# Where the two halves of a split weight chunk and the features start in SBUF: one tile per chunk, placed by the width of the matmuls that use it

## The chip, the cores and the metric

One core of one Trainium2 chip runs the whole program in one launch. The metric is the device time of that core in microseconds (us), the median of several runs. TensorE (PE) multiplies; its weight loads are shown apart as PEld; ScalarE (ACT), VectorE (DVE), GpSimd (POOL) and SyncE (SP, which issues the DMAs) work beside it.

## The reference, cut to what matters

Two blocks of layers on one sequence of 512 tokens with 1024 features, everything in float32:

```python
# first block
x = x + (rms(retention(q, k, v)) * silu(gate)) @ w_out          # 4 heads, after rmsnorm(x) @ w_in
x = x + (softmax_with_sink(q k^T + bias, window 128) v * silu(gate)) @ w_out   # 16 heads ("swa")
# second block, for i in 0, 1
x = layer_norm(ALPHA * x + (mlstm_mixer(x) if i == 0 else pool_mixer(x)))
x = layer_norm(ALPHA * x + memory_cross_attn(x, mem_k, mem_v, wq, wo))
x = layer_norm(ALPHA * x + (relu(x @ w1 + b1) ** 2) @ w2 + b2)   # 1024 -> 4096 -> 1024
```

Nearly all of it are products of [512, 1024] features with weight matrices.

## The kernel before, in words

The features of all 512 tokens lie in SBUF, feature-major, 128 features to a k-tile. Every float32 operand is split into two float32r parts, `hi` (a rounding copy by ACT, L120) and `lo` (the rest, `src - hi`, by DVE, L121), and one product becomes three matmuls (`mm3`, L220 to L222): hi·hi, hi·lo and lo·hi. Each of the three has a weight load (LDWEIGHTS) of 128 columns of its own, so weight load and matmul alternate all through the program: while one matmul streams its moving operand from SBUF, the weight load for the next one reads its stationary operand from SBUF.

Weights come in chunks of one megabyte ([128, 2048] float32). `load` brings a chunk into a `raw` tile by DMA and splits it into a tile `whi` and a tile `wlo` of 8192 bytes per partition each; `chunk` has the next two chunks split ahead of the one in use. `raw` has two places, `whi` and `wlo` three each, taken in turn. During the sliding-window layer one of the three places of `whi` is held for the keys (`kT`).

There are two widths of matmul. In 512-column matmuls the moving operand is either 512 tokens of features (`proj` over the whole sequence: `mm<-xh,whi` in the trace, first the moving and then the stationary operand) or 512 columns of weights (`out_block`, with 128 tokens of features as the stationary operand: `mm<-whi,hh`). In 256-column matmuls it is 256 columns of weights (`tproj`, `mm<-whi,xh`) or half of the tokens (`mm<-xh,whi` with 256). A scheduler sets the order of the instructions on each engine from its own model of their times; tile pools set the addresses.

Where the operands start follows from the built program. All starts here are byte addresses within a partition, modulo 512; every k-tile and every block of 128 columns begins a whole number of 512 bytes further on, so one number stands for a tile:

| Tiles, before | start modulo 512 |
|---|---|
| `whi`, `wlo`, `xh`, `xl`, `kT` | 352 |
| retention's and mLSTM's `q, k, v, p, oh, ol, yh, yl` | 192 |
| the swa layer's `swa_oh, swa_ol, pT, vz` | 288 |
| cross attention's `mk, mv, o01, o23`, `xp`, and the MLP's `hh, hl` | 160 |

"Distance" below means: start of the stationary operand that is loaded during a matmul, less start of the moving operand that this matmul streams, modulo 512. Counted over the built program of before, pair by pair in PE's order, the float32r matmuls have these distances: of 512 columns 2732 at 0, 1912 at 320, 571 at 352 and 196 at 448; of 256 columns 3718 at 0, 211 at 320, 205 at 192 and 140 at 448. The groups in the trace: `mm<-xh,whi` is at 0 in both widths, and so are `mm<-whi,xh` and `mm<-xph,mvh`; `mm<-whi,hh` at 320 with 512 columns and `mm<-whi,o23h` at 320 with 256; `mm<-whi,oh` at 352; `mm<-kT,swa_oh` at 448 and `mm<-o23h,whi` at 192 (both 256).

Of the kernel before, what the change touches and what calls it, by code (L numbers as in the profile page):

```python
# [10 lines left out]
F32 = mybir.dt.float32  # L11
F32R = mybir.dt.float32r
# [3 lines left out]
PSUM = bass.MemoryType.PSUM  # L16

P = 128
# [15 lines left out]
# columns of the packed per-feature vectors  # L34
# [8 lines left out]
# columns of the packed shape-only constants  # L43
# [8 lines left out]

class Ring:
    """a tile pool whose tags hand out their places in turn"""
# [4 lines left out]
    def tile(self, shape, dt, tag, name, bufs=None):  # L59
        n = bufs or self.bufs  # L60
        k = (self.turn.get(tag, -1) + 1) % n
        if k == self.held.get(tag):
            k = (k + 1) % n
        self.turn[tag] = k
        return self.pool.tile(shape, dt, tag=f"{tag}{k}" if n > 1 else tag, name=name, bufs=1)

    def hold(self, shape, dt, tag, name):
        """the next place, kept out of the turns until it is let go"""
        t = self.tile(shape, dt, tag, name)
        self.held[tag] = self.turn[tag]  # L70
        return t

    def let_go(self, tag):
        del self.held[tag]


class Net:
    def __init__(self, ctx, tc, a, out, stop, start):
# [5 lines left out]
        self.wp = pool("w", 3)  # L84
        self.xp = pool("x", 1)
        self.sp = pool("small", 2)
# [4 lines left out]
        # residual stream, token-major  # L91
# [31 lines left out]
    def split_scaled(self, hi, lo, src, sc):  # L123
        """the same of sc * src"""
# [21 lines left out]
    def load(self, name, i, g=None):  # L146
# [4 lines left out]
        elif name == "pool_w":  # column c of group g scaled by pool_scale[g, c]  # L151
            raw, hi, lo = self.wtiles(name, 0)
            sc = self.wp.tile([P, 2048], F32, tag="raw", name="pool_sc", bufs=2)[:, :D]
# [5 lines left out]
        elif g is not None:  # row k * 128 + p scaled by g[p, k]  # L159
# [10 lines left out]
    def order(self, names):  # L170
        """the weight chunks of the phases, in the order of their use"""
# [37 lines left out]
    def wtiles(self, name, i):  # L209
        raw = self.wp.tile([P, 2048], F32, tag="raw", name=self.uid("raw"), bufs=2)  # L210
# [13 lines left out]
    def proj(self, ck, j, x, sl, kt=8, ps=None):  # L224
        """feature-major projection: features j*128.. of the chunk, tokens sl"""
# [7 lines left out]
    def tproj(self, ck, x, blk, ps):  # L233
        """token-major projection of one token block, 256 features of the chunk"""
# [5 lines left out]
    def pow_col(self, col, n, eps):  # L240
        """(col + eps) ** -0.5 for col [128, n]"""
        nc = self.nc
        r = self.sp.tile([P, 32], F32, tag="pow_out", name=self.uid("po"))
        if eps:
            t = self.sp.tile([P, 32], F32, tag="pow_in", name=self.uid("pi"))[:, :n]
# [5 lines left out]
    def bcast_cols(self, cols, w):  # L251
        """per-token columns [128, w/128] -> PSUM [128, w], the same on all partitions"""
# [7 lines left out]
    def rms_cols(self, sq, w, mean, eps):  # L260
        """sq [128, w]: per-partition sums of squares -> the rms factors, as columns"""
# [7 lines left out]
    def add_sq(self, alloc, q, src, w):  # L269
        """q + src^2, a new tile for q None"""  # L270
# [10 lines left out]
    def to_features(self, b, hi, lo):  # L281
        """x of token block b, transposed, as (hi, lo) [128, 8, 128]"""
# [10 lines left out]
    def sumsq_rows(self, src, bias=None):  # L293
        """means of (src + 32 bias)^2 over the rows of src [128, 1024], as two parts of a sum"""
# [9 lines left out]
    def bc_row(self, name, i, pool=None):  # L304
        """row i of a [n, 1024] input on all partitions"""
# [4 lines left out]
    def layer_norm(self, i, b, last, new=True, pool=None, dst=None):  # L310
        """layer norm i of token block b; x holds the residual, self.sm its sums over the features"""
# [29 lines left out]
    def add_to_x(self, b, lo, hi, ps, alpha, acc):  # L341
        """x = alpha x + ps on columns lo..hi of the block; acc: where the row sums go, or None"""
# [4 lines left out]
    def out_block(self, cks, xs, b, c, alpha, acc):  # L347
        """x = alpha x + xs^T W on 512 columns of a token block; cks: per group of 4 k-tiles (hi, lo)"""
# [10 lines left out]
    def out_proj(self, name, base, xs, alpha, after, mid=None):  # L359
        """x = alpha x + xs^T W, K = 1024"""  # L360
# [12 lines left out]
    def group_out(self, name, base, xs, alpha, after=None):  # L373
        """x = alpha x + xs^T W for a group of 4 k-tiles; after: this is the last group"""
# [15 lines left out]
    def retention(self, after):  # L390
# [40 lines left out]
        def theta(ck, nm):  # L431
            """(hi, lo) of the rotated projection, [128, 2 * 512]: even features, odd features"""
# [13 lines left out]
        for h in range(RET_H):  # L446
# [8 lines left out]
            vh, vl = FR(2048, "vh"), FR(2048, "vl")  # [128 tokens, block, 512]  # L455
# [18 lines left out]
            # scores^T with the decay: row block jb of keys, queries from the block on  # L474
# [22 lines left out]
            if last:  # apart from those of the head before, in the place of the last queries and keys  # L497
# [40 lines left out]
    def swa_prelude(self, b):  # L538
        """x1 of token block b as (hi, lo); its rms factor"""
# [9 lines left out]
        # eps of a norm of what the factor has not been applied to: EPS / r^2  # L549
# [3 lines left out]
    def silu_gate(self, ps, out, rb):  # L553
        """2 silu(ps * rb)"""
# [6 lines left out]
    def bias_scratch(self, tp):  # L561
        """DRAM [128, 16, 384], the same for every partition: at distance 255 - column, the bias, or -1e30"""
# [5 lines left out]
        rel = self.sp.tile([32, 16], F32, tag="rel", name="rel", bufs=1)  # L568
# [12 lines left out]
    def swa(self, after):  # L581
# [7 lines left out]
        nsink = p1.tile([P, 2, 8], F32, tag="nsink", name="nsink")  # L589
        sink = p1.tile([P, 2, 8], F32, tag="sink", name="sink")  # L590
# [4 lines left out]
        # ---- keys and values; queries and keys as (hi, lo): two heads' worth of K holds both parts of a head's  # L595
        # queries, against the keys' hi twice, then their lo and zeros
# [4 lines left out]
        kr = self.wp.hold([P, 2048], F32R, tag="whi", name="kT").rearrange("p (x g t) -> p x g t", x=2, g=2)  # L601
# [4 lines left out]
        def normed(ps3, nh, b2):  # L606
            """token-major rows ps3 [128, 2 * nh, 64] times their rms factors -> SBUF, the same shape"""
# [15 lines left out]
        for b2 in range(2):  # L623
# [12 lines left out]
            # token-major, per block and group: hi, hi, then lo, 0  # L636
# [17 lines left out]
        def q_part(c):  # L654
            """q^T of the head pairs 2c, 2c + 1 (heads t, 8 + t on the two halves of the partitions)"""
# [37 lines left out]
        def attend(c, b, bt):  # L693
            """probabilities of the four heads of chunk c for the query block b"""
# [70 lines left out]
        self.wp.let_go("whi")  # L765
# [8 lines left out]
    def mlstm(self, after):  # L774
# [17 lines left out]
        # ---- gates: token-major columns, (block, head)  # L792
# [4 lines left out]
        gb = p1.tile([P, 1], F32, tag="gb", name="gb")  # L797
# [13 lines left out]
        # log sigmoid(f) = min(f, 0) - log1p(exp(-|f|)), log1p(z) = 2 atanh(z / (2 + z))  # L811
# [10 lines left out]
        # cumulative sums within the blocks, their totals, c = i - b  # L822
# [564 lines left out]
```

## Time and profile before

| | |
|---|---|
| time, median of 3 runs (lowest, highest) | 1916.04 us (1914.0, 1916.21) |
| profiled execution, first to last instruction | 1912.8 us |
| PE busy | 1886.2 us, 99% |
| PEld, DVE, ACT busy | 1641.4, 1117.7, 722.2 us |
| DMA share | 27.3% of 16 engines' span |

The span of the profiled execution stands for its own time; the timed runs have some 3 us more around it. A MATMUL's duration in the profile holds the time until its last result has drained, so neighbouring matmuls overlap, and what one matmul costs is the distance from its start to the next one's start, called spacing here. In a stretch without waits the duration is spacing plus a constant: 389 ns go with a spacing of 226.7 ns, 276 ns with 113.3.

### The profile page before, as it was taken

The page shows a single profiled execution, that of the slowest core. Times are in us where ns is not written, and L with a number is a line of the kernel's source. Part 1 is how long each engine was busy: PE and PEld are TensorE (multiplying, and loading weights), DVE is VectorE, ACT ScalarE, POOL GpSimd, SP SyncE. Part 2 cuts the span into 40 slices and gives each one's busy share as a digit, 9 for nine tenths or more (in the row PEclk, how much of TensorE's full clock was granted, in tenths as well). Part 3 has the DMA queues.
Part 4 walks back from the last instruction along what each step waited for, and adds up shares of the span by engine and source line. Part 5 has one row for each costly group of instructions (what it writes and reads, how often), then busy time and mean ns, then how long its engine had stood idle before and what let it go on. Part 6 is the DMA issues. An engine that isn't in the chain of part 4 may idle for free.

```text
span 1912.8 us, 25728 instructions
## 1 busy us (share of the span) xinstructions
PE 1886.2 (99%) x10626; PEld 1641.4 (86%) x10626; DVE 1117.7 (58%) x1942; ACT 722.2 (38%) x1338; POOL 41.6 (2%) x51
## 2 busy tenths in 40 slices
PE   8999999999999999999999999999999999999998
PEld 7888888889888988889998888888899898888886
DVE  5564646467888566646646544444595475444445
ACT  5333223245665344424534332232254353332331
POOL 0000000001010000000000000000000000000000
PEclk9999999999999999999999999999999999999999
DMA  7224221213111321123513323223221233223221
GB/s 262 94 84 149 83 94 67 88 51 108 65 67 56 130 72 66 67 88 111 199 45 117 127 89 109 90 88 107 103 87 50 69 107 119 89 90 108 88 89 44
DMA packets 34037, 182.49 MB, mean 95 GB/s; under 512 B 4032, under 2 KB 8704, under 8 KB 14720
## 3 DMA queue, kind: packets, MB, share of 16 engines
q1 hardware_dynamic: 33920, 180.86, 27.3%
q8 instruction: 83, 1.36, 0.3%
q14 instruction: 34, 0.28, 0.0%
HBM read 178.72 MB, written 5.27 MB: 96 GB/s over the span
## 4 chain that ended last, share of the span: by engine, by line
PE 95%; DVE 3%; ACT 1%; issue 0%; DMA 0%; SPq 0%; DVEq 0%; POOLq 0%; ACTq 0%
PE mm L220 30%; PE mm L222 30%; PE mm L221 30%; PE ax L288 1%; DVE wlo L121 1%; PE ax L221 0%; PE ax L256 0%; PE ax L220 0%; PE ax L222 0%; PE mm L705 0%; ACT whi L120 0%; PE ax L735 0%; PE mm L1182 0%; PE ax L669 0%; PE ax L1051 0%
## 5 line engine op out<-in xcount | busy, mean ns | idle before, releaser
L220 PE MATMUL mm<-xh,whi 128*128 128x512 f32 (+1 forms) x1312 | 463.9, 357 | 7.1 <-ACT xh L129 6.3
L120 ACT CAST whi<-raw 128x1024 fp32r<-128x1024 f32 (+1 forms) x284 | 283.2, 1045 | 494.9 <-PE mm L221 184.0
L221 PE MATMUL mm<-xl,whi 128*128 128x512 f32 (+1 forms) x1312 | 465.7, 356 | 0.0
L222 PE MATMUL mm<-xh,wlo 128*128 128x512 f32 (+1 forms) x1312 | 465.4, 356 | 0.0
L121 DVE TENSOR_TENSOR wlo<-raw,whi 128x1024 fp32r<-128x1024 f32 (+1 forms) x284 | 335.3, 1217 | 174.8 <-ACT whi L120 174.7
L220 PEld LDWEIGHTS mm<-xh,whi 128*128 128x128 f32 x1312 | 247.1, 190 | 42.7 <-ACT xh L129 6.3
L221 PEld LDWEIGHTS mm<-xl,whi 128*128 128x128 f32 x1312 | 248.6, 190 | 34.1 <-DVE xl L130 0.3
L222 PEld LDWEIGHTS mm<-xh,wlo 128*128 128x128 f32 x1312 | 248.5, 189 | 34.2
L344 DVE SCALAR_TENSOR_TENSOR x<-x,mm 128x512 f32<-128x512 f32 x192 | 131.7, 686 | 221.8 <-PE mm L222 221.5
L220 PE MATMUL mm<-whi,hh 128*128 128x512 f32 x512 | 202.6, 396 | 0.0
L221 PE MATMUL mm<-wlo,hh 128*128 128x512 f32 x512 | 202.5, 395 | 0.0
L222 PE MATMUL mm<-whi,hl 128*128 128x512 f32 x512 | 202.5, 395 | 0.0
L220 PE MATMUL mm<-whi,xh 128*128 128x256 f32 x544 | 156.0, 287 | 1.6 <-DVE s L707 0.8
L222 PE MATMUL mm<-whi,xl 128*128 128x256 f32 x544 | 155.2, 285 | 0.1
L221 PE MATMUL mm<-wlo,xh 128*128 128x256 f32 x544 | 154.8, 285 | 0.0
L222 PEld LDWEIGHTS mm<-whi,hl 128*128 128x128 f32 x512 | 96.2, 188 | 23.2
L221 PEld LDWEIGHTS mm<-wlo,hh 128*128 128x128 f32 x512 | 96.3, 188 | 23.1
L220 PEld LDWEIGHTS mm<-whi,hh 128*128 128x128 f32 x512 | 96.3, 188 | 23.0
L220 PEld LDWEIGHTS mm<-whi,xh 128*128 128x128 f32 x544 | 104.9, 193 | 4.1 <-ACT whi L120 1.5
L221 PEld LDWEIGHTS mm<-wlo,xh 128*128 128x128 f32 x544 | 105.0, 193 | 0.3
L222 PEld LDWEIGHTS mm<-whi,xl 128*128 128x128 f32 x544 | 104.9, 193 | 0.3 <-DVE xl L121 0.3
L1119 DVE TENSOR_TENSOR rl<-rl 128x512 f32<-128x512 f32 (+1 forms) x72 | 45.0, 629 | 57.1 <-ACT rl L1117 57.1
(343 smaller groups left out, 2836.8 us busy)
## 6 DMA issues: line engine op xcount, KB each, us to landing
raw<-in_mlp_w_dram SPq DMA_DIRECT2D x64, 1024.0 KB, 4.8
raw<-in_a_w_in_dram SPq DMA_DIRECT2D x23, 1024.0 KB, 5.0
raw<-in_ml_w_in_dram SPq DMA_DIRECT2D x12, 1024.0 KB, 4.8
raw<-in_a_w_out_dram SPq DMA_DIRECT2D x8, 1024.0 KB, 4.9
raw<-in_b_w_in_dram SPq DMA_DIRECT2D x8, 1024.0 KB, 4.9
raw<-in_xa_wq_dram SPq DMA_DIRECT2D x8, 1024.0 KB, 4.8
raw<-in_mem_w_kv_dram SPq DMA_DIRECT2D x8, 1024.0 KB, 4.8
raw<-in_xa_wo_dram SPq DMA_DIRECT2D x8, 1024.0 KB, 5.0
```

The costliest lines, as they stand in the source:

```text
L120: nc.scalar.copy(hi, src)
L121: return nc.vector.tensor_tensor(out=lo, in0=src, in1=hi.bitcast(F32), op=ALU.subtract)
L220: mm(o, a[0], b[0], start=first, stop=False)
L221: mm(o, a[0], b[1], start=False, stop=False)
L222: mm(o, a[1], b[0], start=False, stop=last)
L288: nc.tensor.transpose(ps[:, t * P:(t + 1) * P], self.x[:, b, f:f + P], self.c("ident"))
L344: self.nc.vector.scalar_tensor_tensor(out=x, in0=x, scalar=alpha, in1=ps, op0=ALU.mult, op1=ALU.add, **({} if acc is None else {"accum_out ...
L1119: nc.vector.tensor_tensor(out=u, in0=u, in1=u, op=ALU.mult)
```

## The change

`whi` and `wlo` of a chunk become the two halves of one tile of 4096 + 16 float32 (`w`), of which three exist, each in a pool of its own; `Weights.tile` puts the halves 64 bytes (`STEP`, 16 float32) on or not on from the tile's start, by the tile's place (`level`) and by `half`, which names the chunks that 256-column matmuls use. Small tiles, gaps and the order of pools are chosen so that the features' tiles start at one place modulo 512.

```diff
+STEP = 16
+GAPS = {"ol": 4 * STEP}
...
+class Weights:
+    def __init__(self, pools, level):
+        self.pools, self.level, self.turn, self.held = pools, level, -1, None
+    def tile(self, name, off):
+        self.turn = (self.turn + 1) % len(self.pools)
+        if self.turn == self.held:
+            self.turn = (self.turn + 1) % len(self.pools)
+        k = self.turn
+        t = self.pools[k].tile([P, 4096 + STEP], F32R, tag="w", name=name, bufs=1)
+        o = self.level[k] if not off else STEP - self.level[k]
+        return t[:, o:o + 2048], t[:, o + 2048:o + 4096]
...
+def half(name, i):
+    return (name in ("w_kv", "ml_wg", "mem_w_kv", "xa_wq", "pool_w") or i is not None and (name == "a_w_in" and i % 6 in (2, 3)
+            or name == "b_w_in" and i % 2 == 0 or name == "ml_w_in" and (i == 0 or i % 3 == 1)
+            or name == "mlp_w1" and i % 16 < 2))
...
-        self.wp = pool("w", 3)
+        self.rawp = pool("raw", 2)
+        w = [pool("w0", 1).pool, pool("w1", 1).pool]
+        self.sp = pool("small", 2)
+        self.ws = Weights(w + [pool("w2", 1).pool], (STEP, 0, STEP))
         self.xp = pool("x", 1)
-        self.sp = pool("small", 2)
...
-        hi = self.wp.tile([P, 2048], F32R, tag="whi", name=self.uid("whi"))
-        lo = self.wp.tile([P, 2048], F32R, tag="wlo", name=self.uid("wlo"))
-        return raw, hi, lo
+        return (raw, *self.ws.tile(self.uid("w"), half(name, i)))
...
-        r = rp.tile([P, NB], F32, tag="r", name="r")
+        r = self.cp.tile([P, NB], F32, tag="r", name="r")
...
-        kr = self.wp.hold([P, 2048], F32R, tag="whi", name="kT").rearrange("p (x g t) -> p x g t", x=2, g=2)
+        kr = self.ws.hold("kT", True)[0].rearrange("p (x g t) -> p x g t", x=2, g=2)
...
-        t = lambda sh, tag: self.kvp.tile(sh, F32R, tag=tag, name=tag)
-        self.mk = [t([P, 8, MEM], "mkh"), t([P, 8, MEM], "mkl")]
-        self.mv = [t([P, 2, D], "mvh"), t([P, 2, D], "mvl")]
+        t = lambda n, tag: self.kvp.tile([P, n], F32R, tag=tag, name=tag)
+        mk = [t(STEP + 2048, "mkh")[:, STEP:], t(2048, "mkl")]
+        mv = [t(2048, "mvh"), t(2048 + 128 - STEP, "mvl")[:, :2048]]
```

The same move to the constants' pool as for `r` is made for `sink`, `nsink` and `gb`, and the columns of `pow_col` shrink from 32 to 8.

In the built program of the change all features start at 96 modulo 512; weights for 512-column matmuls start at 96 too, those for 256-column matmuls at 32 or at 160, as do `kT`, `mk`, `mv` and `pT` at 160. The distances, counted as above: of 512 columns 5384 at 0 and some 50 elsewhere; of 256 columns 2417 at 64, 1583 at 448 (that is, 64 below) and 293 at 0; of 384 columns 108 at 0, as before.

No instruction is added or removed on any engine. The scheduler orders some of them anew. On PE 258 of 10465 stand elsewhere, mostly in the swa layer; the MLP's are in the old order. In the swa layer, PE before (a piece in which transposes of queries, `ax<-cst,qx`, and products of probabilities and values, `ax<-pT,vzh`, stand between matmuls of the gate projection, `mm_4804`):

```order
2804 L220 MATMUL mm_4804<-xh_3293,whi_4494 128x512
2805 L221 MATMUL mm_4804<-xl_3294,whi_4494 128x512
2806 L669 MATMUL ax_4644<-cst,qx_4569 128x128 x4
2807 L222 MATMUL mm_4804<-xh_3293,wlo_4495 128x512
2808 L220 MATMUL mm_4804<-xh_3293,whi_4494 128x512
2809 L221 MATMUL ax_4572<-pTl_4594,vzh 128x256
2810 L222 MATMUL ax_4572<-pTh_4593,vzl 128x256
```

The same place in the change, where `mm_4773` is that gate projection:

```order
2799 L257 MATMUL ax_4542<-pTh_4548,vzh 128x256
2800 L258 MATMUL ax_4542<-pTl_4549,vzh 128x256
2801 L259 MATMUL ax_4542<-pTh_4548,vzl 128x256
2802 L706 MATMUL ax_4614<-cst,qx_4539 128x128 x4
2803 L257 MATMUL mm_4773<-xh_3268,w_4465 128x512
2804 L258 MATMUL mm_4773<-xl_3269,w_4465 128x512
```

The transposes have moved ahead of the gate projection and the products of the next probabilities some rows further back. On SP's queue two small loads have moved forward, from the swa and the mLSTM layer to the start of retention. Before:

```order
16 L417 DMA sin<-in_rope_dram 128x512
17 L569 DMA rel<-in_rel_bias_dram 32x16
18 L212 DMA raw_246<-in_a_w_in_dram 128x2048
19 L454 DMA dec_328<-in_decay_dram 128x512
20 L212 DMA raw_254<-in_a_w_in_dram 128x2048
```

In the change:

```order
16 L454 DMA sin<-in_rope_dram 128x512
17 L628 DMA sink<-in_sinks_dram 128x16
18 L251 DMA raw_253<-in_a_w_in_dram 128x2048
19 L835 DMA gb<-in_gate_b_dram 128x1
20 L491 DMA dec_333<-in_decay_dram 128x512
```

One small load stands ahead of the chunk `raw_253` as one did before, and `gb` is one more between the second and the third chunk.

## Rows read from the trace of the kernel before

**Rows 1.** The page: span, busy time by engine, chain that ended last.

```profile
span 1912.8 us, 25728 instructions
...
PE 1886.2 (99%) x10626; PEld 1641.4 (86%) x10626; DVE 1117.7 (58%) x1942; ACT 722.2 (38%) x1338; POOL 41.6 (2%) x51
...
PE 95%; DVE 3%; ACT 1%; issue 0%; DMA 0%; SPq 0%; DVEq 0%; POOLq 0%; ACTq 0%
```

**Rows 2.** Windows, PE: stretch, busy (instructions), granted clock, DMA share, GB/s.

```profile
430.00:577.00 147.00, 140.32 (x984) 0.99 0.23 79
1100.00:1300.00 200.00, 200.00 (x871) 1.00 0.28 95
```

**Rows 3.** Timeline of PE, MLP, first product: start us, duration us, instruction.

```profile
1257.52 0.39 PE L220 MATMUL mm<-xh,whi 128*128 128x512 f32 x1
...
1261.60 0.39 PE L220 MATMUL mm<-xh,whi 128*128 128x512 f32 x1
```

**Rows 4.** Timeline of PE, MLP, second product.

```profile
1223.61 0.40 PE L220 MATMUL mm<-whi,hh 128*128 128x512 f32 x1
...
1234.81 0.40 PE L220 MATMUL mm<-whi,hh 128*128 128x512 f32 x1
```

**Rows 5.** Timeline of PE, retention's output product.

```profile
130.21 0.40 PE L220 MATMUL mm<-whi,oh 128*128 128x512 f32 x1
...
135.83 0.40 PE L220 MATMUL mm<-whi,oh 128*128 128x512 f32 x1
```

**Rows 6.** Timeline of PE, retention's values, 256 columns.

```profile
122.18 0.28 PE L220 MATMUL mm<-whi,xh 128*128 128x256 f32 x1
...
124.70 0.28 PE L220 MATMUL mm<-whi,xh 128*128 128x256 f32 x1
```

**Rows 7.** Timeline of PE, cross attention: keys of the memory, then its values.

```profile
911.82 0.28 PE L221 MATMUL mm<-o23l,whi 128*128 128x256 f32 x1
...
912.88 0.28 PE L221 MATMUL mm<-o23l,whi 128*128 128x256 f32 x1
...
934.81 0.28 PE L221 MATMUL mm<-wlo,o23h 128*128 128x256 f32 x1
...
935.83 0.28 PE L221 MATMUL mm<-wlo,o23h 128*128 128x256 f32 x1
```

**Rows 8.** Timeline of PE, swa scores, at two places.

```profile
472.28 0.50 PE L705 MATMUL mm<-kT,swa_oh 128*128 128x256 f32 x3
...
473.19 0.28 PE L221 MATMUL mm<-wlo,xh 128*128 128x256 f32 x1
...
535.68 0.87 PE L705 MATMUL mm<-kT,swa_oh 128*128 128x256 f32 x6
536.39 0.87 PE L705 MATMUL mm<-kT,swa_ol 128*128 128x256 f32 x6
```

**Rows 9.** Groups of PE by form: count, busy us, mean ns, idle before.

```profile
L220 PE MATMUL mm<-whi,hh 128*128 128x512 f32 x512 | 202.6, 396 | 0.0
L220 PE MATMUL mm<-whi,xh 128*128 128x256 f32 x544 | 156.0, 287 | 1.6 <-DVE s L707 0.8 <-ACT xh L120 0.4 <-DVE vl L130 0.4
L221 PE MATMUL mm<-xl,whi 128*128 128x256 f32 x432 | 121.4, 284 | 0.0
L220 PE MATMUL mm<-whi,oh 128*128 128x512 f32 x96 | 38.2, 398 | 0.0
L221 PE MATMUL mm<-wlo,o23h 128*128 128x256 f32 x64 | 17.7, 276 | 0.0
L221 PE MATMUL mm<-pl,vh 128*128 128x256 f32 x48 | 13.5, 280 | 0.0
```

**Rows 10.** Timeline of PE where the second product ends and the first begins.

```profile
1243.21 0.39 PE L220 MATMUL mm<-xh,whi 128*128 128x512 f32 x1
...
1245.28 0.39 PE L220 MATMUL mm<-xh,whi 128*128 128x512 f32 x1
```

**Rows 11.** Waits: engine, line, awaited: us in total, times, longest.

```profile
ACT whi L120 <- PE mm L221: 184.0, 58, 11.0
...
PE mm L220 <- ACT xh L129: 6.3, 1, 6.3
PE mm L705 <- ACT swa_oh L672: 2.9, 2, 2.5
```

More of the change, by code (lines that the diff above doesn't have):

```diff
@@ L64, in tile, with hold, let_go @@
         self.turn[tag] = k
[L65 to L70, printed above, removed]
-        return t
-    def let_go(self, tag):
-        del self.held[tag]
+        key = f"{tag}{k}" if n > 1 else tag
+        pad = GAPS.get(key, 0) // 4
+        if not pad:
+            return self.pool.tile(shape, dt, tag=key, name=name, bufs=1)
+        w = math.prod(shape[1:])
+        t = self.pool.tile([shape[0], w + pad], dt, tag=key, name=name, bufs=1)[:, :w]
+        return t if len(shape) == 2 else t.rearrange("p (a b) -> p a b", a=shape[1])
+class Weights:
[9 more added lines that the diff above has]
+        return t[:, o:o + 2048], t[:, o + 2048:o + 4096]
+    def hold(self, name, off):
+        t = self.tile(name, off)
+        self.held = self.turn
+        return t
+    def let_go(self):
+        self.held = None
+def half(name, i):
+    return (name in ("w_kv", "ml_wg", "mem_w_kv", "xa_wq", "pool_w") or i is not None and (name == "a_w_in" and i % 6 in (2, 3)
+            or name == "b_w_in" and i % 2 == 0 or name == "ml_w_in" and (i == 0 or i % 3 == 1)
+            or name == "mlp_w1" and i % 16 < 2))
 class Net:
@@ L152, in load @@
             raw, hi, lo = self.wtiles(name, 0)
-            sc = self.wp.tile([P, 2048], F32, tag="raw", name="pool_sc", bufs=2)[:, :D]
+            sc = self.rawp.tile([P, 2048], F32, tag="raw", name="pool_sc")[:, :D]
             self.nc.sync.dma_start(sc, self.a["pool_scale"].to_broadcast([P, D]))
@@ L209, in wtiles @@
     def wtiles(self, name, i):
[L210 removed]
+        raw = self.rawp.tile([P, 2048], F32, tag="raw", name=self.uid("raw"))
         if i is not None:
             self.nc.sync.dma_start(raw, self.a[name][i])
[L213 to L215 removed]
+        return (raw, *self.ws.tile(self.uid("w"), half(name, i)))
     def mm3(self, o, a, b, first, last):
@@ L242, in pow_col @@
         nc = self.nc
-        r = self.sp.tile([P, 32], F32, tag="pow_out", name=self.uid("po"))
+        r = self.sp.tile([P, 8], F32, tag="pow_out", name=self.uid("po"))
         if eps:
-            t = self.sp.tile([P, 32], F32, tag="pow_in", name=self.uid("pi"))[:, :n]
+            t = self.sp.tile([P, 8], F32, tag="pow_in", name=self.uid("pi"))[:, :n]
             nc.vector.tensor_scalar(t, col, float(eps), None, op0=ALU.add)
@@ L567, in bias_scratch @@
         nc.sync.dma_start(ohm[0:16], a["onehot"][0:16, 384:768])
-        rel = self.sp.tile([32, 16], F32, tag="rel", name="rel", bufs=1)
+        rel = self.sp.tile([P, 512], F32, tag="sq", bufs=3, name="rel")[0:32, :16]
         nc.sync.dma_start(rel, a["rel_bias"])
@@ L588, in swa @@
         ident = self.c("ident")
-        nsink = p1.tile([P, 2, 8], F32, tag="nsink", name="nsink")
-        sink = p1.tile([P, 2, 8], F32, tag="sink", name="sink")
+        nsink = self.cp.tile([P, 2, 8], F32, tag="nsink", name="nsink")
+        sink = self.cp.tile([P, 2, 8], F32, tag="sink", name="sink")
         nc.sync.dma_start(sink.rearrange("p g h -> p (g h)"), a["sinks"])
@@ L796, in mlstm @@
         nc.sync.dma_start(mask, a["tri"][1])
-        gb = p1.tile([P, 1], F32, tag="gb", name="gb")
+        gb = self.cp.tile([P, 1], F32, tag="gb", name="gb")
         nc.sync.dma_start(gb, a["gate_b"])
```

6 lines of the change are left out of this document (4 added, 2 removed).

## Prediction

> **What bounds the kernel now.** I read the page first: PE is busy for 1886.2 of 1912.8 us, and 95% of the chain that ended last is PE's own work [rows 1]. Then the windows: in the MLP PE is busy for all of 200 us at full granted clock, so nothing there waits for memory or for another engine; in the swa layer PE idles for 6.7 of 147 us [rows 2]. So the time is the sum of PE's spacings, and a change that adds and removes no instruction can only act through the spacing of a matmul, or through the waits, which are few: the list of waits has PE's first at 6.3 us, once, at the start, and 2.9 us in swa [rows 11].
>
> Then the timeline, for the spacing itself, over long stretches without a wait. The same instruction on the same shape does not always cost the same. With 512 columns, the MLP's first product has 18 matmuls from 1257.52 to 1261.60, 226.7 ns each [rows 3]; the second product 48 from 1223.61 to 1234.81, 233.3 ns [rows 4]; retention's output product 24 from 130.21 to 135.83, 234.2 ns [rows 5]. With 256 columns, retention's values have 21 from 122.18 to 124.70, 120.0 ns [rows 6]; in cross attention 9 from 911.82 to 912.88 take 117.8 ns and 9 from 934.81 to 935.83 take 113.3 [rows 7].
>
> Now set these beside the table of distances. At 512 columns the cheap stretch is at distance 0, the dear ones at 320 and 352. At 256 columns it is the other way round: 120.0 at distance 0, 117.8 at 192, 113.3 at 320. At 448 the scores of swa take 8 matmuls from 472.28 to 473.19, 113.8 ns each, at one place, and 6 from 535.68 to 536.39, 118.3 ns, at another [rows 8]: here the same distance has two spacings. The one follows 256-column matmuls, the other 512-column ones, so it looks as if the spacing settled into one of two steady patterns by what went before. I read this as the weight load for the next matmul and the moving stream of this one getting in each other's way in SBUF, by where they stand to each other.
>
> **A rule that speaks against this.** The rows show 226.7, 233.3 and 234.2 ns for one shape at one granted clock [rows 3 to 5]. The Trainium skill, "TensorE: Matmul & The Clock Gate", section "Step-by-step: what each phase is for", has two independent SBUF read ports on PE, one for the moving operand and one for the weight load, so that loading the next weights takes nothing from the running matmul; "SBUF — State Buffer", section "Who interferes with whom", has PE wait on nobody. By this rule the distance does nothing and the time stays at 1916. The rows contradict the rule at least in that something other than the shape sets the spacing; that it is the distance is my inference, and the rule stands below as a rival.
>
> **The change part by part.**
>
> *512 columns.* Nearly all go to distance 0, at 96 and 96 instead of 352 and 352. That is the case of rows 3, moved by 256 bytes on both sides; 226.7 ns is taken. The 1912 at 320 save 6.67 ns each [rows 3, 4], 12.8 us (1536 of them are the MLP's, x512 three times [rows 9]); the 571 at 352 (288 of them retention's output product, x96 three times [rows 9]) save 7.5 ns [rows 3, 5], 4.3 us; the 196 at 448 have no clean row with 512 columns and get 4 ns, between nothing and 6.67: 0.8 us. Together 17.9 us. Bounds of the unsure part: 0 and 1.3 us.
>
> *256 columns, what they cost today above the cheapest pattern, 113.3 ns.* 3120 matmuls of the 3718 at distance 0 (x544 and x432, three times each, and 192 of cross attention) at 120.0: 6.67 ns each, 20.8 us [rows 6, 9]. The other 600, of retention, mLSTM and swa, show a duration of 280 ns against 276 for 113.3 and come to about 118: 4.7 ns, 2.8 us [rows 9]. The 205 at 192: 4.5 ns, 0.9 us [rows 7]. The 140 at 448: between 113.8 and 118.3, 0.5 us [rows 8]. The 211 at 320 nothing. Sum 25.0 us.
>
> *256 columns in the change.* 2417 stand at 64. No row of before is at 64; the nearest by placement is 320, which is 64 and half of 512, at 113.3 [rows 7]. The bounds are 113.3 and 120.0, the ends of all 256-column rows. I take 113.3: rows 7's other stretch, 192, and the swa scores at 448 also differ by half of 512 and agree at 118, so half of 512 looks like no difference. 1583 stand at 448, where 113.8 and 118.3 were both seen [rows 8]; I take 117.8, since most chunks of this kind follow 512-column products, as did the scores that took 118: 4.5 ns, 7.1 us. The 293 at 0 stay at about 119.3: 1.8 us. Together 8.9 us, a gain of 16.1 us. With all 4000 at 113.3 the gain is 23.2; with all at 117.8 it is 5.2; with all at 120.0 it is a loss of 3.5.
>
> *Settling.* Where the distance changes, some matmuls pass before the pattern is steady: after the second product 9 matmuls take 2.07 us, 0.03 more than 9 times 226.7 [rows 10]. With some 60 such changes of width (an estimate from the layers' structure) this is 2 us that my steady spacings leave out, taken off the gain.
>
> *One tile for both halves.* ACT writes `hi` and DVE `lo` of a chunk two chunks ahead, and it is ACT that waits for PE to free a place (184.0 us over 58 times), not PE for ACT [rows 11]. If the whole tile now comes free only after the last matmul on either half, ACT starts one matmul later, 0.2 us, which that wait hides; if the cover were gone, a chunk's conversion would stand on the path. I cost it at nothing. The two small loads moved on SP pass no chunk that PE waits for, since PE's list has no wait for a chunk after the start: nothing, or some tenths of a microsecond at the start.
>
> *Order.* The swa layer has 6.7 us of PE idle time [rows 2], of which 2.9 us are the scores' waits for the queries [rows 11], whose transposes now stand earlier. That may be worth anything from a gain of 3 us to a loss of 3; I take nothing.
>
> **Sum.** 17.9 + 16.1 - 2.0 = 32.0 us. 1912.8 less 32.0 is 1880.8 for the span; the timed median lies 3.2 us above the profiled span today, so 1884.
>
> **Rivals.**
>
> - *Both signs of 64 are cheap* (113.3 for all 4000): 17.9 + 23.2 - 2 = 39.1, 1877. For it: 113.8 was seen at 448, too [rows 8]. Against: it was the rarer pattern, after 256-column matmuls. 0.20.
> - *Both settle at 117.8*: 17.9 + 5.2 - 2 = 21.1, 1895. For it: 192 and 448 both mostly do [rows 7, 8], and 64 is unmeasured. 0.17.
> - *64 costs as much as 0 at 256 columns* (120.0): 17.9 - 3.5 - 2 = 12.4, 1904. 0.07.
> - *The change doesn't do what it says*: the spacing goes with the role of the operands, or with the region of SBUF, and not with the distance; the rule above would say so. 1916. Against: role doesn't explain it, since weights move and features stand still in rows 6 and 7's last, with 120.0 and 113.3. Region might. 0.07.
> - *Slower: a third pattern at 64, dearer than 120.* 39.1 us are there if all 4000 take 113.3, so the change loses once their mean is above 113.3 + 39.1 / 4.0 = 123.1 ns. At 126.7, as far above 120.0 as that is above 113.3, it is 1930. For it: 64 is unmeasured, and spacing does depend on distance in steps. Against: no steady row of 256 columns is above 120. 0.05.
> - The forecast itself has 0.40; 0.04 is left for a worse order in swa and what I don't see.
>
> **How the numbers follow.** Forecast alone: 1880 to 1889, with the order's 3 us and the parts above. The range takes in the first two rivals with the order's 3 us on the low side and 5 on the high: 1873 to 1900. Beyond it lie 120.0, no effect and slower. A measurement of this kernel can tell about 0.2%, 4 us. Faster by more: the forecast, the first three rivals and most of the rest, 0.87; within: no effect, 0.07; slower: 0.06.
>
> **What would show it.** In the profile of the changed kernel, the MLP's second product should show a duration of 389 ns instead of 396, as the first does, and the window from 1100 to 1300 some 1.5% more matmuls. Retention's values and the cross attention's projections of 256 columns should fall from 282 to 276 in some chunks and to 280 in others, in turn with the tile's place. PE's waits should be as now. I would be wrong if 512-column matmuls at 96 and 96 did not take 226.7, if 256-column stretches at 64 showed 280 or more, or if swa's idle time grew by several microseconds.

## The result, and the profile after

| | before | changed |
|---|---|---|
| time, median (lowest, highest) | 1915.24 us (1914.0, 1916.21), 4 runs | 1887.99 us (1887.29, 1889.82), 4 runs |
| profiled execution, span | 1912.8 us | 1886.2 us |
| PE busy | 1886.2 us | 1856.7 us |

The ratio is 0.9859, with a 95% interval of 0.9845 to 0.9873: 27 us faster, 4 us above the forecast of 1884 and inside its range. An execution's time lies 1.8 us above its span here (1888.0 and 1886.2); the 3.2 us of the prediction set the median before, 1916.04, beside the span of one execution. Measured once more beside other kernels, on another occasion (run e10 below), the changed kernel took 1887.09 us against 1916.16, with a span of 1884.3.

The page of the changed kernel, with the lines that answer to [rows 1]: span, busy time by engine, and the chain that ended last.

```profile
span 1886.2 us, 25702 instructions
...
PE 1856.7 (98%) x10626; PEld 1627.5 (86%) x10626; DVE 1115.2 (59%) x1942; ACT 721.0 (38%) x1338; POOL 40.2 (2%) x51
...
PE 95%; DVE 3%; ACT 1%; DMA 0%; issue 0%; SPq 0%; DVEq 0%; POOLq 0%; POOL 0%; ACTq 0%
```

PE has the same 10626 instructions and is busy 29.5 us less; DVE, ACT and POOL are nearly as before. The bound is the same, only its spacings are shorter. The groups of PE by form, as in [rows 9]: count, busy us, mean ns, idle before.

```profile
L257 PE MATMUL mm<-xh,w 128*128 128x512 f32 x880 | 345.4, 394 | 6.6 <-ACT xh L168 6.6
L257 PE MATMUL mm<-w,hh 128*128 128x512 f32 x512 | 199.3, 389 | 0.0
L257 PE MATMUL mm<-w,xh 128*128 128x256 f32 x544 | 153.4, 282 | 0.9 <-ACT xh L159 0.4 <-DVE vl L169 0.4
L258 PE MATMUL mm<-xl,w 128*128 128x256 f32 x432 | 119.0, 279 | 0.0
```

The MLP's second product is at 389 ns where it was at 396; the 256-column groups fell from 287 and 284 to 282 and 279. 276 and 280 stand for the two patterns of 256 columns; the group with the mean of 282 has 201 of its 544 matmuls at 276 and 304 at 279 to 281, and its mean is raised by a few long ones at breaks. Windows of PE at the places of [rows 2], the swa layer and the MLP: stretch, busy (instructions), granted clock, DMA share, GB/s.

```profile
424.00:570.00 146.00, 137.37 (x974) 0.99 0.24 79
1086.00:1286.00 200.00, 200.00 (x884) 1.00 0.28 97
```

884 matmuls fit in 200 us of the MLP where 871 did, 1.5% more. In the swa layer PE now idles for 8.6 us of 146, where it did for 6.7 of 147. The list of waits, as in [rows 11]: engine, line, awaited: us in total, times, longest.

```profile
PE mm L742 <- ACT swa_oh L709: 7.0, 3, 2.8
PE mm L257 <- ACT xh L168: 6.6, 1, 6.6
```

The scores' wait for the queries (`swa_oh`) has grown from 2.9 to 7.0 us. That was not forecast.

**Where the time went, from the starts of all matmuls in the two traces.** I took each spacing between neighbours and put it beside 226.67 ns for 512 columns and 113.33 for 256. Spacings up to 262 and 150 ns hold what the distance and the settling cost; longer ones have a wait or other work in them and are called breaks here.

| above the cheapest spacing, us | before | changed |
|---|---|---|
| 512 columns, no break | 19.8 | 2.9 |
| 256 columns, no break | 24.7 | 10.7 |
| breaks | 27.1 | 32.2 (29.8 in the second profile, e10) |
| the float32 matmuls, all of their spacing | 87.4 | 86.4 |

So the placement is worth 16.9 + 14.0 = 30.9 us, of which 3 to 5 are lost again in breaks, and 1.0 is won at the float32 matmuls.

Some of the breaks are made by TensorE's clock. Inside the span it falls now and then from its upper level (granted clock 1.00, 2.4 GHz) to its lower one (0.50, 1.2 GHz): once in the profile before, at 514.1 us, a moment after PE had waited 1.40 us; twice in the first profile of the change, at 531.6 us, after the wait of 2.74 us for `swa_oh`, and at 681.8 us, after 1.9 us of small float32 products. Windows of PE at the last of these places, during the fall and behind it: stretch, busy (instructions), granted clock, DMA share, GB/s.

```profile
681.90:684.90 3.00, 3.00 (x9) 0.50 0.00 0
689.50:692.50 3.00, 3.00 (x15) 1.00 0.00 0
```

512-column matmuls at 0 start some 426 ns apart in the first window and some 228 in the second, and this fall, which lasts until 685.2 us, costs 1.7 us. The second profile of the change has two falls as well (489.1 and 530.0 us), both in the swa layer.

### The profile page after: what moved, and what is told of

The parts are those of the page before. It is cut to its first block, busy times and chain, and to the rows that moved or that the text cites. A ratio compares the mean times of both kernels' runs of the same rounds, so it can differ in the third digit from the quotient of the medians.

```text
span 1886.2 us, 25702 instructions
## 1 busy us (share of the span) xinstructions
PE 1856.7 (98%) x10626; PEld 1627.5 (86%) x10626; DVE 1115.2 (59%) x1942; ACT 721.0 (38%) x1338; POOL 40.2 (2%) x51
## 4 chain that ended last, share of the span: by engine, by line
PE 95%; DVE 3%; ACT 1%; DMA 0%; issue 0%; SPq 0%; DVEq 0%; POOLq 0%; POOL 0%; ACTq 0%
PE mm L257 30%; PE mm L259 30%; PE mm L258 30%; PE ax L325 1%; DVE w L160 1%; PE ax L257 0%; PE ax L293 0%; PE ax L258 0%; PE ax L259 0%; PE ax L772 0%; PE mm L742 0%; PE ax L1091 0%; ACT w L168 0%; PE ax L706 0%; PE mm L1222 0%
## 5 line engine op out<-in xcount | busy, mean ns | idle before, releaser
L257 PE MATMUL mm<-xh,w 128*128 128x512 f32 (+1 forms) x1312 | 462.4, 356 | 7.4 <-ACT xh L168 6.6
L258 PE MATMUL mm<-xl,w 128*128 128x512 f32 (+1 forms) x1312 | 463.5, 354 | 0.0
L259 PE MATMUL mm<-xh,w 128*128 128x512 f32 (+1 forms) x1312 | 463.4, 354 | 0.0
L159 ACT CAST w<-raw 128x1024 fp32r<-128x1024 f32 (+1 forms) x284 | 282.8, 1043 | 436.2 <-PE mm L259 269.5
L160 DVE TENSOR_TENSOR w<-raw,w 128x1024 fp32r<-128x1024 f32 (+1 forms) x284 | 337.0, 1216 | 130.6 <-ACT w L159 130.5
L257 PEld LDWEIGHTS mm<-xh,w 128*128 128x128 f32 x1312 | 246.1, 189 | 42.7 <-ACT xh L168 6.6
L259 PEld LDWEIGHTS mm<-xh,w 128*128 128x128 f32 x1312 | 247.3, 189 | 34.4
L258 PEld LDWEIGHTS mm<-xl,w 128*128 128x128 f32 x1312 | 247.3, 189 | 34.3 <-DVE xl L169 0.3
L257 PE MATMUL mm<-w,hh 128*128 128x512 f32 x512 | 199.3, 389 | 0.0
L258 PE MATMUL mm<-w,hh 128*128 128x512 f32 x512 | 199.2, 389 | 0.0
L259 PE MATMUL mm<-w,hl 128*128 128x512 f32 x512 | 199.2, 389 | 0.0
L257 PE MATMUL mm<-w,xh 128*128 128x256 f32 x544 | 153.4, 282 | 0.9 <-ACT xh L159 0.4
L258 PE MATMUL mm<-w,xh 128*128 128x256 f32 x544 | 152.3, 280 | 0.0
L257 PEld LDWEIGHTS mm<-w,hh 128*128 128x128 f32 x512 | 96.1, 188 | 19.8
L257 PEld LDWEIGHTS mm<-w,xh 128*128 128x128 f32 x544 | 102.9, 189 | 3.8 <-ACT pre L914 2.3
L258 PEld LDWEIGHTS mm<-w,xh 128*128 128x128 f32 x544 | 102.6, 189 | 0.2
```

The costliest lines, as they stand in the source:

```text
L159: nc.scalar.copy(hi, src)
L160: return nc.vector.tensor_tensor(out=lo, in0=src, in1=hi.bitcast(F32), op=ALU.subtract)
L257: mm(o, a[0], b[0], start=first, stop=False)
L258: mm(o, a[0], b[1], start=False, stop=False)
L259: mm(o, a[1], b[0], start=False, stop=last)
```

## The experiments

**e1: is it the distance?** Before, with one edit: an unused tile of 192 bytes ahead of the MLP's pool. It moves `hh` and `hl` from 160 to 352, so that the second product is at distance 0 and the first, as before, too. Weights, order and one tile or two stay as before.

```diff
+        self.pool(es, "gap", 1).tile([P, 48], F32, tag="gap", name=self.uid("gap"))
         p2 = self.pool(es, "mlp", 2)
```

> The kernel before, with an unused tile of 192 bytes ahead of the MLP's pool, so that the hidden features start at 352 modulo 512 like the weights; nothing else moves (weights keep two tiles each, order as before). Distance theory: the 1536 matmuls of the MLP's second product go from 320 to 0, their spacing from 233.3 to 226.7 ns and their duration from 396 to 389, 10.2 us off the kernel before, about 1905. Rival (role of the operands or region of SBUF sets the spacing): 396 stays, about 1915.

1903.6 us against 1916.32, ratio 0.9938 (0.9923 to 0.9953): 12.7 us faster. The group of the second product, which answers to [rows 9]:

```profile
L220 PE MATMUL mm<-whi,hh 128*128 128x512 f32 x512 | 199.4, 389 | 0.0
```

396 became 389. Only a start address moved. The rival in which the distance does nothing falls: the spacing of this product went from 233.3 to 226.7 ns. The Trainium skill, "TensorE: Matmul & The Clock Gate", section "Step-by-step: what each phase is for", says that loading the next weights takes no SBUF read bandwidth from the running matmul. If nothing else tied the two together, the start of `hh` could not matter, and here it does. The weight loads of this product take 188 ns before and in e1; what in the chip lengthens the spacing is not shown by any run.

**e2: at what period does it repeat?** The same edit with 64 bytes of gap in the first MLP and 448 in the second, which puts the second products at 384 and at 256.

```diff
+        self.pool(es, "gap", 1).tile([P, (16, 112)[l]], F32, tag="gap", name=self.uid("gap"))
```

> The kernel before, with an unused tile of 64 bytes ahead of the MLP's pool in layer 0 and of 448 bytes in layer 1: the second product stands at distance 384 (128 below 0) in layer 0 and at 256 in layer 1. If the spacing repeats every 128 bytes of distance, both layers take 226.7 ns (duration 389) and the time is about 1905, as with the gap of 192. If it repeats every 256 bytes, only layer 1 does, about 1910. If only every 512 bytes, neither need be at 389; with durations of 396 the time is about 1915.

1910.28 us, ratio 0.9967 (0.9953 to 0.9981). The group in a window in the first MLP (distance 384), then one in the second (256):

```profile
L220 PE MATMUL mm<-whi,hh 128*128 128x512 f32 x171 | 67.5, 395 | 0.0
...
L220 PE MATMUL mm<-whi,hh 128*128 128x512 f32 x193 | 75.1, 389 | 0.0
```

256 is as cheap as 0, and 384, which is 128 modulo 256, is not. So at 512 columns 256 counts as 0, as the prediction had supposed for 64 and 320 at 256 columns; that every distance repeats after 256 bytes is not shown by this, and e5 has a case against it.

**e3 and e4: what does placing by width give?** The changed kernel with one place for all weights: 96 (distance 0 for both widths), or 32 and 160 (64 and 448 for both).

```diff
-        return (raw, *self.ws.tile(self.uid("w"), half(name, i)))
+        return (raw, *self.ws.tile(self.uid("w"), False))   # e3; e4: True
```

> The changed kernel with every weight chunk placed as for 512 columns, so that the 256-column matmuls with weights (some 3660 of 4300) stand at distance 0. Distance theory: they take 120.0 ns again instead of a mean of some 115.5, 3400 more than now at 0 by 4.5 ns is 15 us, about 1903; 512 columns stay at 389. Rival (the shared tile, the order or the region made the gain): about 1888. The swa layer's idle time tells the new order from the faster matmuls: 8.6 us if the order made it, back near 6.7 if it was the matmuls getting faster than what they wait for.

> The changed kernel with every weight chunk placed as for 256 columns, so that 5244 of the 512-column matmuls stand 64 above or below 0. Distance theory: 233.3 ns instead of 226.7, as at 320 before, 35 us more, about 1923; if the cheaper pattern of 229 ns that 448 had here and there before is the common one, 12 us more, about 1900. 256 columns stay. Rival (region, tile sharing or order): about 1888.

e3 took 1900.41 us (ratio 0.9919, 0.9904 to 0.9933), e4 1907.45 (0.9956, 0.9941 to 0.9971). Both beat the kernel before, and the changed kernel, which places by width, is 12 and 19 us below them. Of e3, a 256-column group:

```profile
L257 PE MATMUL mm<-w,xh 128*128 128x256 f32 x544 | 155.5, 286 | 0.9 <-ACT xh L159 0.4 <-DVE vl L169 0.4
```

and of e4, the same group and the MLP's second product:

```profile
L257 PE MATMUL mm<-w,xh 128*128 128x256 f32 x544 | 153.4, 282 | 0.9 <-ACT xh L159 0.4 <-DVE vl L169 0.4
L257 PE MATMUL mm<-w,hh 128*128 128x512 f32 x512 | 201.3, 393 | 0.0
L259 PE MATMUL mm<-w,hl 128*128 128x512 f32 x512 | 202.2, 395 | 0.0
```

The group means 286 against 282 and 389 against 393 to 395 say that the best distance of one width is a bad one of the other. e4 lies between its two forecasts because the signs are not alike at 512 columns: from the starts, 233.2 ns at 64 and 229 to 230 at 448. The start of one operand alone is not the cause either: features at 96 as the stationary operand go with 227 ns in the changed kernel, where the moving weights start at 96, and with 229 to 233 in e4, where they start at 32 or 160.

**e5 and e6: a scan of the distance in steps of 16 bytes.** The changed kernel with tiles of 4096 + 36 float32, in which each chunk is put on by 0 to 144 bytes in turn; e6 has another turn, so that other layers meet a distance.

```diff
...
+        self.n += 1
-        o = self.level[k] if not off else STEP - self.level[k]
+        o = 4 * (3 * self.n % 10)   # e6: 4 * ((7 * self.n + self.n // 10) % 10)
...
```

> A scan, meant to be read from the timeline and not from its time: the changed kernel with weight tiles 80 bytes wider each and each chunk put at a place of its own, 16 bytes apart, by a count over the chunks, so that distances of every multiple of 16 occur, taken modulo 256 (the earlier run had 226.7 ns at a distance of 256 as at 0). Distance theory: matmuls of one width at one distance have one or two spacings, whichever chunk, layer or place in SBUF they belong to; with 512 columns 226.7 at 0, 229 to 233 at 64 and 192, about 232 at 128; with 256 columns 120 at 0, 113.3 or 117.8 at 64 and 192. Time about 1910. Rival (the place in SBUF or the layer matters beside the distance): one distance shows spacings that go with the layer or the place. If a distance is found at which 256 columns always take 113.3, a kernel better than the changed one follows.

> The same scan with another count, so that the same distances fall on other chunks: the distances of scan a should have the same spacings here if the distance sets them, others if it is the chunk or layer. Which of two steady patterns a stretch takes may differ between the two scans, since what comes before it differs. Time about 1910.

One run each: 1920.8 and 1923.02 us, beside 1914.46 of before, where about 1910 was expected. What counts here is the spacing in the settled part of each long stretch, by distance modulo 256, from the starts, for nine of the sixteen distances:

| distance | 512 columns, ns | 256 columns, ns |
|---|---|---|
| 0 | 226.7, always | 120.0 |
| 16 | 226.7, 233.3 or 236.6 | 117.2 |
| 64 | 233.3 | 113.3 or 117.8 |
| 96 | 234.3 | 117.3 or 118.6 |
| 128 | 232.4 or 233.3 | 118.6 |
| 144 | 231 or 233.3 | 113.4 with the weights moving, 116.7 or 120.0 with the features moving |
| 160 | 233.3 | 120.0 |
| 192 | 228.9 or 233.3 | 113.4 or 117.8 |
| 240 | 226.7, 228.3 or 231.7 | 116.7 to 120.2 |

Of e5, groups by form of PE in three stretches: one at 0, and two at 16 with the same operands at two places in the MLP. Modulo 512 they are at 256, 272 and 16.

```profile
L258 PE MATMUL mm<-w,hh 128*128 128x512 f32 x13 | 5.1, 389 | 0.0
...
L258 PE MATMUL mm<-w,hh 128*128 128x512 f32 x13 | 5.2, 400 | 0.0
...
L258 PE MATMUL mm<-w,hh 128*128 128x512 f32 x13 | 5.0, 388 | 0.0
```

The second settles at 236.6 ns (400), the third at 226.7 (388, as at distance 0). But these two differ by 256 in their distance, and of such stretches with the weights moving the two scans have two at 272, both at 236.6, and two at 16, both at 226.7. So 256 bytes may be what makes the difference here, and one row of the table can hide two distances. Two spacings also occur where the distance modulo 512 and the starts modulo 512 are the same. Of e5, two stretches of 256 columns with the features moving, both at 400 (144 modulo 256):

```profile
L259 PE MATMUL mm<-xl,w 128*128 128x256 f32 x11 | 3.0, 279 | 0.0
...
L259 PE MATMUL mm<-xl,w 128*128 128x256 f32 x11 | 3.1, 284 | 0.0
```

From the starts these are 116.7 and 120.0 ns. So the distance gives a small set of steady patterns, and something else chooses among them. Of e6, a stretch at 144 with the weights moving:

```profile
L259 PE MATMUL mm<-w,o23h 128*128 128x256 f32 x14 | 3.9, 276 | 0.0
```

**e7: 144 for the weights that move.** In one of the three places the chunks whose weights move in 256-column matmuls start at 208 modulo 256. PE's order is that of the change. The edit moves more than that: all other weights that move in 256-column matmuls go to 64, among them the 336 that were at 448, and 658 matmuls whose features move go from 64 to 448.

```diff
...
-        o = self.level[k] if not off else STEP - self.level[k]
+        o = ((0, 16, 28), (32, 16, 16), (32, 16, 16))[k][off]
...
```

(`off` is 2 for the chunks whose weights move in 256-column matmuls, and the tiles are 4096 + 32 float32.)

> The changed kernel, but in one of the three places of the weight tile the chunks whose weights move in 256-column matmuls start at 208 instead of 32 modulo 256, which puts 1145 of these matmuls at distance 144; of the 2359 in the changed kernel's trace the others stay at 64 or 192. PE's order is the same. Theory A: at 144, with the weights moving, there is only the pattern of 113.3 ns, which the scan showed in four stretches out of four. The changed kernel's weights-moving matmuls lie 6.3 us above 113.3 ns; some 3 us of this goes, and the time is about 1885. Theory B: 144 has two patterns as 64 has, and what goes before chooses; then the mean of the 1145 stays at 115 to 118 ns and the time at 1887 to 1889.

1886.25 us (ratio 0.9849, 0.9835 to 0.9864), beside 1887.09 for the changed kernel on the same chip: no difference that can be measured. Theory A is right on the pattern, as every long stretch at 144 ended at 113.4 ns, and wrong on the worth: the stretches begin with some twelve matmuls between 114 and 123 ns, and the mean over the 1114 at 144 without a break is 114.9, where the changed kernel has 115.4 at 64 with the weights moving. The time is not the worth of 144 alone, though. By the starts, the matmuls whose weights move went from 4.8 to 2.8 us above 113.3 ns each, and the other 256-column ones, many of which the same edit moved, from 6.0 to 6.7.

**e8: do the two halves in one tile cost something?** e3 with `hi` and `lo` in two tiles again, at the same addresses.

```diff
...
+        hi = self.pools[k].tile([P, 2048 + o], F32R, tag="hi", name=name + "h", bufs=1)
+        lo = self.pools[k].tile([P, 2048 + STEP - o], F32R, tag="lo", name=name + "l", bufs=1)
+        return hi[:, o:], lo[:, :2048]
...
```

> The kernel with all weights at 96, but hi and lo of a chunk in two tiles again, at the same addresses. In the kernel with all weights at 96 PE waits 7.0 us for swa_oh in three places, as in the changed kernel, against 2.9 us before. Theory A: these waits come from the order, which the scheduler made anew because the two halves share one tile; with two tiles the order is nearly that of before, the wait falls back to about 3 us and the time from 1900.4 to about 1896.5. Theory B: the waits come from the matmuls that have become faster while the queries' chain on DVE and ACT has not; then they stay at 7 us and the time within 2 us of 1900.4.

1901.41 us (ratio 0.9927, 0.991 to 0.9944), not below e3's 1900.41. The order is nearly that of before again: 25 of PE's 10465 instructions stand elsewhere than before, where in the change, and in e3, it is 258. (Some 120 more of its 256-column matmuls are at distance 0 instead of 448, since the keys come to lie in another place: 120 times some 2 ns, 0.2 us.) The list of waits of e3:

```profile
PE mm L742 <- ACT swa_oh L709: 7.0, 3, 2.8
```

and of e8:

```profile
PE mm L743 <- ACT swa_oh L710: 2.9, 2, 2.5
PE ax L258 <- DVE ou L783: 1.9, 2, 1.4
PE mm L260 <- DVE o23l L161: 1.5, 2, 0.8
PE ax L773 <- DVE pTl L161: 1.4, 1, 1.4
```

Theory A holds for the wait: with one tile the scheduler orders the swa layer anew, and with that the wait became 7.0 us. (Whether the order alone does it, or the dependences that come with the one tile, is not separated.) It fails for the time. The old order has other waits and cuts the products into more pieces: summed over the starts, the breaks take 28.4 us in e8 and 29.3 in e3, and the float32 matmuls 87.9 and 86.5. TensorE's clock falls three times inside the span of e8's profile and twice in e3's. The two orders cost the same within what can be measured.

**e9: what chooses the pattern?** The changed kernel with one 128x128 float32 matmul ahead of each of retention's eight stretches of 96 value products.

```diff
+                        if not b2 and not b:
+                            nc.tensor.matmul(ps[:, 0, :P], self.c("ident"), self.c("ident"), start=True, stop=True)
                         self.tproj(ck, xs, b2 * 2 + b, ps[:, b, :])
```

> The changed kernel, with one 128x128 float32 matmul added ahead of each of the eight stretches of 96 value products in retention (its result is overwritten). In the changed kernel five of these stretches, at 64 and at 192, run at 117.7 ns from the first to the last matmul, three of them right behind 512-column matmuls; one runs at 113.4. Theory A: what goes before chooses the pattern; with the added matmul most of the five fall to 113.4, 0.4 us each, and the time falls by some 1 us, less 8 added matmuls of about 0.15 us. Theory B: distance and place alone choose; the five stay at 117.7, and the time rises by 1 us.

One run: 1886.17 us. Ahead of the six later stretches PE's order is that of the change but for the added matmul; some 100 instructions stand elsewhere than in the change, most of them in the swa layer, so the time does not weigh the added matmuls. Of the changed kernel, the first and the last of 96 matmuls in three stretches (timeline of PE: start, duration, instruction), two at 64 and one at 448; the first and the third stand behind 512-column matmuls, the second behind 256-column ones:

```profile
112.56 0.28 PE L257 MATMUL mm<-w,xh 128*128 128x256 f32 x1
...
123.75 0.28 PE L259 MATMUL mm<-w,xl 128*128 128x256 f32 x1
...
150.45 0.29 PE L257 MATMUL mm<-w,xh 128*128 128x256 f32 x1
...
161.24 0.28 PE L259 MATMUL mm<-w,xl 128*128 128x256 f32 x1
...
214.44 0.28 PE L257 MATMUL mm<-w,xh 128*128 128x256 f32 x1
...
225.64 0.28 PE L259 MATMUL mm<-w,xl 128*128 128x256 f32 x1
```

and the same three of e9:

```profile
111.57 0.37 PE L257 MATMUL mm<-w,xh 128*128 128x256 f32 x1
...
122.43 0.28 PE L259 MATMUL mm<-w,xl 128*128 128x256 f32 x1
...
149.28 0.36 PE L257 MATMUL mm<-w,xh 128*128 128x256 f32 x1
...
160.55 0.28 PE L259 MATMUL mm<-w,xl 128*128 128x256 f32 x1
...
213.90 0.36 PE L257 MATMUL mm<-w,xh 128*128 128x256 f32 x1
...
225.17 0.28 PE L259 MATMUL mm<-w,xl 128*128 128x256 f32 x1
```

95 spacings are 11.19, 10.79 and 11.20 us in the changed kernel, so 117.8, 113.6 and 117.9 ns; in e9 they are 10.86, 11.27 and 11.27, the settling behind the added matmul with them. One stretch at 64 fell to the cheap pattern, and so did a third one at 64 (from 315.72 us); the other rose to the dear one. The choice is not chance: in e10, the changed kernel once more, all six stretches of 96 have the same means as in its first profile, to a tenth of a nanosecond. What goes before does choose, in both directions, at 64. The three stretches at 448 all stayed at 117.7. Both theories had a part of it.

**e11: is it the sign, then?** e9 with all weights that move in 256-column matmuls at 32, so at 64 (or 320) and none at 448. The same edit takes 658 matmuls whose features move from 64 to 448.

```diff
...
+        t = self.pools[k].tile([P, 4096 + (16, 80, 16)[k]], F32R, tag="w", name=name, bufs=1)
+        o = ((16, 0, 0), (0, 16, 48), (16, 0, 0))[k][off]
...
```

> The kernel with the float32 matmul added ahead of retention's value products, and the weights that move in 256-column matmuls at 32 in every place, so that they stand at 64 and none of them at 192 (the tile of the second place is 256 bytes longer; PE's order is that of the kernel with the added matmul). There the stretches at 64 behind 512-column matmuls fell to 113.4 ns, and the three at 192 stayed at 117.7. Theory A: with the weights moving, the sign decides whether the cheap pattern can be reached; the three stretches, now at 64, fall to 113.4 behind the added matmul where 512-column matmuls stood ahead, and some of the keys' products fall too. That is 1 to 3 us: 1884 to 1887. Theory B: the place in the program decides, and the three stay at 117.7: 1886 to 1888.

1885.77 us (1884.37 to 1886.24), ratio 0.9845 (0.9831 to 0.9858). The third stretch above and the last, which was at 448 too:

```profile
213.94 0.37 PE L263 MATMUL mm<-w,xh 128*128 128x256 f32 x1
...
224.80 0.28 PE L265 MATMUL mm<-w,xl 128*128 128x256 f32 x1
...
330.97 0.37 PE L263 MATMUL mm<-w,xh 128*128 128x256 f32 x1
...
341.84 0.28 PE L265 MATMUL mm<-w,xl 128*128 128x256 f32 x1
```

10.86 and 10.87 us, the cheap pattern; the other stretch that had been at 448, from 250.68 to 261.95, stayed at 117.7, behind 256-column products at distance 0, as the one from 149.28 in e9. e7 has the same three stretches at 64 without an added matmul: there two of them, from 250.09 and from 329.46 us, settle at 113.3, and the one behind 512-column matmuls stays at 117.8. So with moving weights in retention the sign decides whether the cheap pattern is to be had, and what goes before whether it is taken. In the median this is 1 to 2 us below the changed kernel, within the intervals, and its profile has one fall of the clock inside the span where those of the changed kernel have two: no version was found that measurably beats it.

**e10** is the changed kernel again, beside e7, e8 and e9.

> The changed kernel as it is, beside the others on the same chip: 1888 within 2 us.

1887.09 us (1884.27 to 1888.1), ratio 0.9848 (0.9834 to 0.9863).

## Why the prediction was right, and where it was not

*The distance as the cause*: right, and shown by e1, which changes nothing but an address. Region of SBUF and role of the operand fall as causes of the 6.7 ns. *Settled patterns*: right, shown by e5, e9 and e11.

*512 columns, 17.9 us*: 16.9 measured, and the settling at 512 columns is in that. e1 moves the 1536 matmuls of the MLP alone, 6.67 ns each and 10.2 us by the sum: its span is 1901.9, 10.9 us less, and its median 12.7 us less. By the starts, its 512-column matmuls without a break stand 9.3 us above the cheapest spacing, where they were at 19.8; so 10 to 11 us are the second product's, and the other 2 us of the median are no more than executions of one kernel differ by (1914.0 to 1916.21 us before). *256 columns and settling, 16.1 - 2.0 = 14.1*: 14.0 measured. How the 2.0 us of settling divide between the widths, the prediction did not say; together 32.0 us were forecast and 30.9 measured.

*The step that failed* is the one on how 64 and 448 differ: "2417 stand at 64 ... I take 113.3" and "1583 stand at 448 ... I take 117.8, since most chunks of this kind follow 512-column products". In the changed kernel the means without a break are, at 64, 115.4 ns with the weights moving and 115.0 with the features; at 448, 117.5 with the weights (or the keys, the memory's keys and the probabilities, which are counted with them) and 115.2 with the features. The 64 was taken too low by 2 ns, the 448 with moving features too high by 2.6; only the 448 with moving weights was met. In sums, nothing was forecast at 64 and 4.5 us measured, and 7.1 were forecast at 448 and 4.6 measured. That the total fits (8.9 + 2.0 for settling = 10.9 us forecast above the cheapest pattern, 10.7 measured) is luck: the errors cancel. 113.3 is not the spacing of a distance but of a pattern which a stretch takes or misses by what went before it (e9). The rival in which both signs are cheap was wrong for the same reason. That the weight load and the moving stream get in each other's way in SBUF stays an inference: the runs show that the spacing goes with the difference of the two starts, not by what means.

*Order, "I take nothing"*: right in the time, by e8 against e3. *"PE's waits should be as now"*: wrong; the scores' wait went from 2.9 to 7.0 us, with the new order (e8), and swa's idle time, which the prediction names as a way to be wrong, rose from 6.7 to 8.6 us.

*One tile at nothing*: the waits of ACT for a free place are hidden, as said, but the tile was also what gave the scheduler other dependences and so another order (e8); the prediction had these as two separate edits.

*Why 1888 and not 1884.* The sum was 32.0 us off the span; the first profile shows 26.6 and the second 28.5. Of the placement 1.1 us is missing, and the breaks grew by 5.1 or 2.7 us, against 1.0 won at the float32 matmuls. The 5.4 us that the first profile lacks, less the 1.4 by which the step from span to median was put too high (3.2 and 1.8), are the 4 us. On the dear side stand the longer wait for the queries, 4.1 us, and a second fall of the clock, up to 1.7, neither of which the prediction reckoned with; some other waits became shorter. The same kernel's breaks differ by 2.4 us between two executions, and the order by itself showed nothing that can be measured, so what part of their growth belongs to the change stays open.

## What to carry to other kernels

When weight load and matmul alternate without a wait, look at start-to-start spacings of one shape at different places of the program, and set them beside the start addresses of what is loaded and what is streamed. A pad of 192 bytes was worth 10 to 11 us of PE's time here (12.7 us in the medians), and the best distance differs by the width of the matmul, so operands may have to be placed by their use. The cheapest spacing seen at a distance is not what all stretches take: cost a placement with the mean over stretches with different work ahead of them.

## What the runs showed of the hardware that was not expected

- The spacing of a float32r matmul goes with the distance between the starts of stationary and moving operand (e1 to e6): at 512 columns from 226.7 ns at 0 to 236.6 at 272, at 256 columns from 113.3 to 120.0, with one stretch of e6 at 123.4 at distance 304. 256 counts as 0 (e2), but with the weights moving 16 and 272 did not behave alike, at 226.7 and 236.6 ns in two stretches each (e5, e6).
- A distance has one to three steady patterns, and a single added 128x128 float32 matmul switches a whole stretch of 96 from one to the other, either way (e9).
- At 144 all long stretches with moving weights settled at 113.4 ns, but took some twelve matmuls to settle (e7); with moving features it was 116.7 or 120.0 (e5, e6).
- The granted clock fell to half for a short stretch once to three times inside the span, behind waits or small float32 products where it was looked at; one fall among 512-column matmuls cost 1.7 us.
